# An MLP's first product by seven block products instead of eight, on one core

## The chip, the core and the metric

The program runs on one core of a Trainium2 chip. The metric is the device time of one execution in microseconds (us). The engines named below are PE (TensorE, the matrix multiplier; PEld is its weight load), DVE (VectorE), ACT (ScalarE), POOL (GpSimd) and SP (SyncE, which here only issues DMAs). Each runs its own instructions in order and waits on semaphores for the others. 16 DMA engines move the data, whoever issues a transfer.

## The reference, cut to what matters

The program is two transformer blocks, in float32. The first has two layers, each with a mixer and an MLP. The change touches the MLPs alone:

```python
def squared_relu_mlp(h, w_up, w_down):
    a = jax.nn.relu(jnp.einsum('bld,df->blf', h, w_up))
    return jnp.einsum('blf,fd->bld', a * a, w_down)

# in first_block, once per layer
h = h + squared_relu_mlp(rmsnorm(h, mlp_norm[layer]), w_mlp_up[layer], w_mlp_down[layer])
```

`h` has 528 tokens (16 of them meta tokens) of 1024 features, `w_up` is 1024 x 4096, `w_down` 4096 x 1024. Layer 0 (first mixer: a gated scan over chunks beside latent attention) computes all 528 tokens; in layer 1 (second mixer: a pooling over windows) only 512 are needed.

## The kernel before, in words

Everything is held transposed: features on the 128 partitions, tokens along the free dimension, so `h` is eight tiles of 128 x 528. A float32 product is made of three float32r products: an operand is split into `hi` (a rounding cast, on ACT) and `lo` (the rest, `x - hi`, on DVE), and hi x hi, hi x lo and lo x hi are accumulated in PSUM. `split` (L258 to L262) does this for weights: `whi` is written at L259 and `wlo` at L260.

The weights of all products lie in one packed DRAM tensor, `stream`, in pieces of 512 KB (eight 128 x 128 blocks). `hu` (L212) loads a piece from the SP queue (`load`, L253) into one of three `raw` buffers and splits it into one of three `whi` and three `wlo` buffers. `dense` (L270, its matmuls at L289) multiplies a piece with `xh` and `xl`; with 528 tokens each weight block is used for two halves of 264 columns (`pm`, a pair of PSUM banks), with 512 tokens for one matmul of 512 columns (`ps`).

`mlp` (L1082) runs once per layer. It splits the eight tiles of `h` into `xh` and `xl` (`xsplit`, L466 and L467), starts the first two column blocks of `w_up`, and computes the rms row `rb` beside them (`rms`, L413 and L417; the row is made at L427 to L453). Then four groups run: eight column blocks of `w_up` (32 in all), each followed by ReLU times `rb` on DVE (L1108), a square on ACT (L1112) and a split into `ah` and `al`, and then eight column blocks of `w_down`, whose results are added to `h` on DVE (L1121). For layer 1 the tiles of `h` are first finished by `pool_band` (L1184 ff.), one tile at a time.

Layer 0's mixer (`layer0`, L574) is woven of threads in six phases (`WEAVES`). At the start of the second phase POOL fetches a table of masks, `msk` (L634), DVE turns it into bytes (L635), and each of the four scan heads uses it (`att_level`, L561). POOL also clears a few tiles in this stage (L514, L945, L1063, L1069).

A scheduler places the instructions of each engine: program order is only a priority, and an instruction that is ready goes ahead of an earlier one that is not.

## Time and profile before

| | us |
|---|---|
| median of 3 runs | 1750.56 (1749.06 to 1750.74) |
| the profiled execution | 1750.7 |
| its span, first to last instruction | 1748.8 |
| layer 0's MLP, from its first full column block to the last group's end | 341.6 to 711.2 |
| layer 1's MLP, the same | 749.2 to 1102.2 |

The profile's page gives busy times of the engines over the whole span. Its views by stage are the chain of work that ended last (what ended each wait, followed back from the end), the table of busy times in stretches of the span, the timeline of an engine (start, duration, tile written and tiles read), the groups of like instructions with their count and mean duration, and the DMA queues and transfers of a stretch. The granted clock of PE is 1.00 (2.4 GHz) through both MLPs.

### The profile page before, as it was taken

The page shows a single profiled execution, that of the slowest core. Times are in us where ns is not written, and L with a number is a line of the kernel's source. Part 1 is how long each engine was busy: PE and PEld are TensorE (multiplying, and loading weights), DVE is VectorE, ACT ScalarE, POOL GpSimd, SP SyncE. Part 2 cuts the span into 40 slices and gives each one's busy share as a digit, 9 for nine tenths or more (in the row PEclk, how much of TensorE's full clock was granted, in tenths as well). Part 3 has the DMA queues.
Part 4 walks back from the last instruction along what each step waited for, and adds up shares of the span by engine and source line. Part 5 has one row for each costly group of instructions (what it writes and reads, how often), then busy time and mean ns, then how long its engine had stood idle before and what let it go on. Part 6 is the DMA issues. An engine that isn't in the chain of part 4 may idle for free.

```text
span 1748.8 us, 26901 instructions
## 1 busy us (share of the span) xinstructions
PE 1700.9 (97%) x10674; PEld 1494.4 (85%) x10674; DVE 1090.7 (62%) x1885; ACT 860.5 (49%) x1419; POOL 54.5 (3%) x66
## 2 busy tenths in 40 slices
PE   8999999999999999999999999999999999999996
PEld 7999999999999999878888888767767788888884
DVE  7677675643434344553434345589867768999996
ACT  5456654432323133541413134454346359999995
POOL 0000000000000000000000000100000000101111
PEclk9999999999999999999999999999989999999999
DMA  5211113332323232133333334322201468999994
GB/s 190 70 50 49 37 37 106 85 96 86 94 88 94 89 91 79 61 91 93 94 97 96 96 97 135 111 73 73 73 13 55 160 224 292 348 339 377 374 375 136
DMA packets 72482, 228.42 MB, mean 131 GB/s; under 512 B 8456, under 2 KB 8512, under 8 KB 72352
## 3 DMA queue, kind: packets, MB, share of 16 engines
q1 hardware_dynamic: 69120, 216.22, 36.4%
q0 software_dynamic: 3232, 10.44, 3.0%
q8 instruction: 85, 1.39, 0.3%
q14 instruction: 45, 0.37, 0.1%
HBM read 213.50 MB, written 13.12 MB: 130 GB/s over the span
## 4 chain that ended last, share of the span: by engine, by line
PE 92%; DVE 5%; ACT 2%; issue 1%; DMA 0%; SPq 0%; POOL 0%; POOLq 0%; DVEq 0%; ACTq 0%
PE pm L289 32%; PE ps L289 29%; PE ps L1591 7%; PE ps L1571 3%; PE ps L266 3%; PE ps L267 2%; PE ps L268 2%; PE ps L557 2%; PE ps L2062 1%; DVE wlo L260 1%; PE ps L2037 1%; PE ps L1192 1%; PE pm L485 1%; PE ps L2055 1%; DVE acc L1837 1%
## 5 line engine op out<-in xcount | busy, mean ns | idle before, releaser
L259 ACT CAST whi<-wraw 128x1024 fp32r<-128x1024 f32 (+1 forms) x309 | 321.3, 1045 | 606.6 <-PE pm L289 293.1
L260 DVE TENSOR_TENSOR wlo<-wraw,whi 128x1024 fp32r<-128x1024 f32 (+1 forms) x309 | 373.4, 1217 | 42.5 <-ACT whi L259 32.3
L289 PE MATMUL pm<-xh,whi 128*128 128x264 f32 x976 | 202.2, 288 | 8.7 <-ACT whi L259 5.9
L289 PE MATMUL pm<-xh,wlo 128*128 128x264 f32 x976 | 200.9, 287 | 0.5 <-DVE wlo L260 0.5
L289 PE MATMUL pm<-xl,whi 128*128 128x264 f32 x976 | 200.6, 287 | 0.0
L289 PE MATMUL ps<-xh,whi 128*128 128x512 f32 x472 | 192.1, 407 | 0.0
L289 PE MATMUL ps<-xh,wlo 128*128 128x512 f32 x472 | 186.2, 395 | 0.0
L289 PE MATMUL ps<-xl,whi 128*128 128x512 f32 x472 | 185.5, 393 | 0.0
L289 PEld LDWEIGHTS pm<-xh,whi 128*128 128x128 f32 x976 | 152.8, 190 | 9.8 <-ACT whi L259 5.9
L289 PEld LDWEIGHTS pm<-xh,wlo 128*128 128x128 f32 x976 | 152.7, 190 | 0.8 <-DVE wlo L260 0.7
L289 PEld LDWEIGHTS pm<-xl,whi 128*128 128x128 f32 x976 | 152.2, 189 | 0.4 <-DVE xl L467 0.3
L289 PEld LDWEIGHTS ps<-xh,whi 128*128 128x128 f32 x472 | 89.3, 189 | 23.6 <-issue 1.8
L289 PEld LDWEIGHTS ps<-xh,wlo 128*128 128x128 f32 x472 | 89.1, 189 | 21.0
L289 PEld LDWEIGHTS ps<-xl,whi 128*128 128x128 f32 x472 | 89.3, 189 | 19.4 <-issue 0.5
L1591 PE MATMUL ps<-wlo,xg 128*128 128x512 f32 x256 | 103.8, 406 | 1.7 <-DVE wlo L260 1.6
L289 PE MATMUL pm<-ah,whi 128*128 128x264 f32 x512 | 104.2, 285 | 0.0
L289 PE MATMUL pm<-ah,wlo 128*128 128x264 f32 x512 | 104.0, 285 | 0.0
L1591 PE MATMUL ps<-whi,xg 128*128 128x512 f32 x256 | 103.7, 405 | 0.0
L289 PE MATMUL pm<-al,whi 128*128 128x264 f32 x512 | 103.7, 284 | 0.0
L289 PE MATMUL ps<-ah,whi 128*128 128x512 f32 x256 | 101.1, 395 | 0.0
L289 PE MATMUL ps<-ah,wlo 128*128 128x512 f32 x256 | 101.0, 394 | 0.0
L289 PE MATMUL ps<-al,whi 128*128 128x512 f32 x256 | 100.5, 393 | 0.0
(501 smaller groups left out, 3202.4 us busy)
## 6 DMA issues: line engine op xcount, KB each, us to landing
wraw<-in_stream_dram SPq DMA_DIRECT2D x306, 512.0 KB, 3.6
t<-in_stream_dram SPq DMA_DIRECT2D x90, 256.0 KB, 6.9
h<-in_stream_dram SPq DMA_DIRECT2D x37, 512.0 KB, 6.0
h<-in_xT_dram SPq DMA_DIRECT2D x16, 264.0 KB, 4.3
hd<-h SPq DMA_DIRECT2D x8, 256.0 KB, 2.0
h<-hd SPq DMA_DIRECT2D x8, 256.0 KB, 4.2
out_dram<-t SPq DMA_DIRECT2D x8, 256.0 KB, 2.3
gt<-rbd POOLq DMA_DIRECT2D x4, 256.0 KB, 5.6
```

The costliest lines, as they stand in the source:

```text
L259: self.nc.scalar.copy(hi, src)
L260: i = self.nc.vector.tensor_sub(lo, src, hi.bitcast(F32))
L266: nc.tensor.matmul(ps, wh, xh, start=start, stop=False)
L267: nc.tensor.matmul(ps, wh, xl, start=False, stop=False)
L268: nc.tensor.matmul(ps, wl, xh, start=False, stop=stop)
L289: nc.tensor.matmul(ps, w[:, b, :], x[:, sl], start=(first and f and i == 0), stop=(last and l and i == nb - 1))
L485: nc.tensor.matmul(pm[:, s, :H2], l, r[:, s * H2:(s + 1) * H2], start=i == 0, stop=i == len(pairs) - 1)
L557: nc.tensor.matmul(pa[:, j * 64:(j + 1) * 64], xs, self.second(xs, i), start=True, stop=True)
L1192: nc.tensor.matmul(ps[:, i * 128:i * 128 + n], self.z[:, i, cols], self.bands[i][:, g, :n], start=False, stop=i == NT - 1, skip_group_chec ...
L1571: nc.tensor.matmul(pg[:, j * m:(j + 1) * m], src[2 * i + k // 4][:, sl], oh[:, i, :m], start=i == 0, stop=i == NT - 1, skip_group_check=True)
L1591: nc.tensor.matmul(pa, xk, v[:, k], start=kk == 0 and n == 0, stop=kk == 7 and n == 1, skip_group_check=True)
L1837: nc.vector.match_replace(out=acc, in_to_replace=m8, in_values=acc, imm_value=sel)
```

## The change

The up-product of each MLP is computed by one level of Strassen's scheme. Features, columns and tokens are halved: for each pair of column blocks (16 pairs of 2 x 128 columns) the eight block products of (half of the features) x (half of the tokens) become seven, of which three use a plain quarter of `w_up` and four use a sum or difference of quarters. One such product (`up_prod`) is 12 matmuls of 264 columns (256 in layer 1).

- The four sums of weights (`up_sums`) are formed in a DRAM tensor for all pairs at once, by DMAs that POOL issues: four copies of a quarter (4 MB each), then four DMAs that add into them, some of which read the result of an earlier one. Layer 0's are written into the program at the starts of the mixer's second to fifth phase, layer 1's at the starts of the four groups of layer 0's MLP.
- `up_weights` loads the seven operands of each pair from the two DRAM tensors in pieces of 256 KB, two to a `raw` buffer, and splits them as before.
- `up_x` makes the seven token-side operands (scaled halves of `h`, their sums and differences), each split into `hi` and `lo`, in four steps between which the first pair's products are issued.
- `pair` runs seven products in two to four PSUM banks. Partial sums that several outputs need are copied out of the accumulating bank by ACT while the bank goes on accumulating, and are added on DVE.
- `dense` puts the two halves of 264 columns in two single banks, since layer 0's MLP now runs with eight single PSUM banks. `w_down` is multiplied as before.

```diff
-N_DENSE = 198
+N_DENSE = 198 - 2 * 32
+UP_PARTS = (("w", 0), ("s", 0), ("s", 1), ("w", 1), ("s", 2), ("s", 3), ("w", 3))
+PAIRS = 16
 def pack_stream(i, hus):
...
+def pack_up(w):
+    v = w.reshape(2, 4, 128, PAIRS, 2, 128)
+    return np.ascontiguousarray(v.transpose(4, 0, 3, 2, 1, 5)).reshape(4, PAIRS, 128, 4, 128)
 def shape_consts():
...
+        elif n == T and self.p_pm is None:
+            res = [self.psb()[:, :H2] for _ in range(2)]
+            parts = [(res[s], slice(s * H2, (s + 1) * H2)) for s in range(2)]
...
+        self.ups = {}
+        sums = self.up_sums(0)
...
                     nc.gpsimd.dma_start(msk, self.a["msk"])
                     nc.vector.tensor_copy(self.msk, msk)
+                if n:
+                    next(sums, None)
                 self.weave(*[(thread(th), m) for th, m in ws])
...
+    def up_sums(self, layer):
+        up = self.a["up%d" % layer]
+        s = self.ups[layer] = self.p_d.tile([4, PAIRS, 128, 4, 128], F32, name="ups%d" % layer)
+        for j, q in ((0, 2), (2, 0), (1, 0), (3, 1)):
+            self.nc.gpsimd.dma_start(s[j], up[q])
+        yield
+        for some in (((0, up[3]), (2, up[2])), ((1, s[0]),), ((3, s[1]),)):
+            for j, src in some:
+                self.nc.gpsimd.dma_start(s[j], src, accum_op=OP.add, max_dma_last_dim=8192)
+            yield
+    def up_weights(self, layer):
+        src = {"w": self.a["up%d" % layer], "s": self.ups[layer]}
+        seq = [(t, q, p) for p in range(PAIRS) for t, q in UP_PARTS]
+        for j in range(0, len(seq), 2):
+            raw = self.p_raw.tile([128, 8, 128], F32, name="wraw")
+            for b in range(2):
+                t, q, p = seq[j + b]
+                self.nc.sync.dma_start(raw[:, 4 * b:4 * b + 4], src[t][q, p])
+            hi = self.p_whi.tile([128, 8, 128], F32R, name="whi")
+            lo = self.p_wlo.tile([128, 8, 128], F32R, name="wlo")
+            self.split(hi, lo, raw)
+            for b in range(2):
+                yield hi[:, 4 * b:4 * b + 4], lo[:, 4 * b:4 * b + 4]
+    def up_x(self, pa, h, gname, n, ready):
+        nc = self.nc
+        hn = n // 2
+        x = {p: [None] * 4 for p in range(7)}
+        left = []
+        def half():
+            if not left:
+                big = len(self.bx) < 8
+                t = [(self.p_x if big else pa).tile([128, T], F32R, name=nm if big else "b" + nm, bufs=None if big else 6)
+                     for nm in ("xh", "xl")]
+                self.bx.append(t)
+                left.extend([[v[:, s * hn:(s + 1) * hn] for v in t] for s in range(2)])
+            return left.pop(0)
+        def put(p, k, src, scale=None):
+            hi, lo = half()
+            if scale is None:
+                nc.scalar.copy(hi, src)
+                nc.vector.tensor_sub(lo, src, hi.bitcast(F32))
+            else:
+                nc.scalar.activation(hi, src, AF.Copy, scale=scale)
+                nc.vector.scalar_tensor_tensor(lo, src, scale, hi.bitcast(F32), op0=OP.mult, op1=OP.subtract)
+            x[p][k] = hi, lo
+        self.bx = []
+        tops, bots, n6 = {}, {}, {}
+        for k in range(4):
+            ready(k)
+            b = tops[k] = pa.tile([128, T], F32, name="ah")[:, :n]
+            nc.scalar.activation(b, h[k], AF.Copy, scale=self.vec(gname, k))
+            put(0, k, b[:, :hn])
+        yield x
+        for k in range(4):
+            b = tops[k]
+            nc.vector.tensor_sub(b[:, :hn], b[:, :hn], b[:, hn:])
+            put(1, k, b[:, :hn])
+        for k in range(4):
+            ready(4 + k)
+            b = bots[k] = pa.tile([128, T], F32, name="al")[:, :n]
+            nc.scalar.activation(b, h[4 + k], AF.Copy, scale=self.vec(gname, 4 + k))
+            t = tops[k]
+            nc.vector.tensor_add(t[:, :hn], t[:, :hn], b[:, hn:])
+            put(2, k, t[:, :hn], -1.0)
+        yield x
+        for k in range(4):
+            put(3, k, bots[k][:, :hn])
+        for k in range(4):
+            t = tops[k]
+            nc.vector.tensor_sub(t[:, hn:], bots[k][:, hn:], t[:, hn:])
+            put(4, k, t[:, hn:])
+        yield x
+        for k in range(4):
+            put(5, k, bots[k][:, hn:])
+        for k in range(4):
+            t = tops[k]
+            nc.vector.tensor_sub(t[:, :hn], t[:, :hn], bots[k][:, :hn])
+            put(6, k, t[:, :hn])
+        yield x
+    def up_prod(self, ps, w, x, hn, first, last):
+        nc = self.nc
+        (hi, lo) = next(w)
+        for k, (xh, xl) in enumerate(x):
+            for v, y, f, l in ((hi, xh, True, False), (hi, xl, False, False), (lo, xh, False, True)):
+                nc.tensor.matmul(ps, v[:, k, :], y, start=first and f and k == 0, stop=last and l and k == 3, skip_group_check=True)
     def mlp(self, h, layer, n, ready=lambda c: None, done=lambda c: None):
         nc, tc = self.nc, self.tc
+        hn = n // 2
         with ExitStack() as es:
-            pa = es.enter_context(tc.tile_pool(name="mlp", bufs=12))
+            pa = es.enter_context(tc.tile_pool(name="mlp", bufs=8))
             b8 = list(range(8))
-            up = [self.hu(cols("up%d" % layer, j * 128)) for j in range(3)]
-            xh, xl = self.xsplit(h, "mlp%d" % layer, n, ready)
-            w = [up.pop()]
-            up[0] = self.dense(up[0], b8, xh, xl, n)
-            acc = self.dense(up[1], b8[:4], xh[:4], xl[:4], n, None, True, False)
-
-            def rest():
-                up[1] = self.dense(up[1], b8[4:], xh[4:], xl[4:], n, acc, False, True)[0]
-
-            rb, _ = self.rms(h, n, rest)
-            rbv = self.v2(rb) if n == T else rb
+            w = self.up_weights(layer)
+            xs = self.up_x(pa, h, "mlp%d" % layer, n, ready)
+            def pair(x):
+                u, c = (self.psb()[:, :hn] for _ in range(2))
+                p1, q = self.tmp(n), self.tmp(n)
+                p1sb, usb, u7sb = p1[:, :hn], p1[:, hn:], q[:, :hn]
+                prod = lambda ps, p, f, l: self.up_prod(ps, w, x[p], hn, f, l)
+                prod(u, 0, True, False)
+                nc.scalar.copy(p1sb, u)
+                yield
+                prod(c, 1, True, True)
+                prod(u, 2, False, False)
+                nc.scalar.copy(usb, u)
+                yield
+                a = self.psb()[:, :hn]
+                prod(a, 3, True, True)
+                prod(u, 4, False, False)
+                nc.scalar.copy(u7sb, u)
+                t = [self.tmp(n) for _ in range(2)]
+                nc.vector.tensor_add(t[0][:, :hn], a, p1sb)
+                nc.vector.tensor_add(t[0][:, hn:], c, usb)
+                nc.vector.tensor_add(t[1][:, hn:], c, u7sb)
+                yield
+                d = self.psb()[:, :hn]
+                prod(d, 5, True, True)
+                prod(u, 6, False, True)
+                nc.vector.tensor_add(t[0][:, hn:], d, t[0][:, hn:])
+                def rest(rb):
+                    rbv = [rb[:, s * hn:(s + 1) * hn] for s in range(2)]
+                    stt = nc.vector.scalar_tensor_tensor
+                    stt(t[1][:, :hn], u, 0.0, rbv[0], op0=OP.min, op1=OP.mult)
+                    stt(t[1][:, hn:], t[1][:, hn:], 0.0, rbv[1], op0=OP.min, op1=OP.mult)
+                    stt(t[0], t[0], 0.0, rb, op0=OP.max, op1=OP.mult)
+                    for v in t:
+                        b = self.tmp(n)
+                        nc.scalar.activation(b, v, AF.Square)
+                        hi = pa.tile([128, T], F32R, name="ah")[:, :n]
+                        lo = pa.tile([128, T], F32R, name="al")[:, :n]
+                        self.split(hi, lo, b)
+                        ah.append(hi)
+                        al.append(lo)
+                yield rest
+            x, it, rb = None, None, None
+            sums = iter(()) if layer else self.up_sums(1)
             for g in range(4):
+                next(sums, None)
                 ah, al = [], []
-                for j in range(8):
-                    if up:
-                        pm = up.pop(0)
+                for j in range(4):
+                    if it is None:
+                        it = x and pair(x)
+                    if g == 0 and j == 0:
+                        for _ in range(4):
+                            x = next(xs)
+                            if _ == 0:
+                                it = pair(x)
+                            rest = next(it)
+                        it = None
+                        def mid():
+                            nonlocal it
+                            it = pair(x)
+                            for _ in range(2):
+                                next(it)
+                        rb, _ = self.rms(h, n, mid)
                     else:
-                        pm = self.dense(w.pop(0) if w else self.hu(cols("up%d" % layer, (g * 8 + j) * 128)), b8, xh, xl, n)
-                    t = self.tmp(n)
-                    tv = self.v2(t) if n == T else t
-                    nc.vector.scalar_tensor_tensor(tv, pm, 0.0, rbv, op0=OP.max, op1=OP.mult)
-                    if g == 0 and j == 1:
-                        w.append(self.hu(cols("up%d" % layer, 384), pin=True))
-                    a = self.tmp(n)
-                    nc.scalar.activation(a, t, AF.Square)
-                    hi = pa.tile([128, T], F32R, name="ah")[:, :n]
-                    lo = pa.tile([128, T], F32R, name="al")[:, :n]
-                    self.split(hi, lo, a)
-                    ah.append(hi)
-                    al.append(lo)
+                        for rest in it:
+                            pass
+                        it = None
+                    rest(rb)
                 for c in range(8):
                     pm = self.dense(self.hu(cols("down%d" % layer, c * 128, 8, g * 8)), b8, ah, al, n)
-                    hk = self.v2(h[c]) if n == T else h[c]
-                    nc.vector.tensor_add(hk, hk, pm)
+                    for hk, p in zip([h[c][:, :hn], h[c][:, hn:]], pm) if n == T else [(h[c], pm)]:
+                        nc.vector.tensor_add(hk, hk, p)
                     if g == 3:
                         done(c)
             return
         with self.tc.tile_pool(name="pool", bufs=1) as p:
             self.pool_begin(p)
+            self.banks(0, 8)
             self.mlp(self.h, 0, T, done=self.pool_part)
             for k in range(8):
                 self.dump("h_mlp0", self.h[k], lambda d, k=k: d[:, k, :])
             if self.stop == "mlp0":
                 return
             self.pool_layer(p)
-            self.banks(0, 8)
             hr = [self.h[k][:, NM:] for k in range(8)]
             self.mlp(hr, 1, S, ready=self.pool_band)
         for k in range(8):
```

## Rows read from the trace of the kernel before

**Rows 1.** The page's head: span, then busy time (share of the span).
```profile
span 1748.8 us, 26901 instructions
PE 1700.9 (97%) x10674; PEld 1494.4 (85%) x10674; DVE 1090.7 (62%) x1885; ACT 860.5 (49%) x1419; POOL 54.5 (3%) x66
```
**Rows 2.** Chain that ended last, in order of time: start, duration, what.
```profile
341.64 338.96 PE pm L289 x2784
...
749.23 352.96 PE ps L289 x1524
```
**Rows 3.** By stretch: busy PE, PEld, DVE, ACT, POOL; clock, DMA share, GB/s.
```profile
322.00:341.50 19.50, 18.05 (x150) 17.81 (x148) 14.99 (x28) 12.13 (x19) 0.00 (x0) 1.00 0.20 55
341.60:386.50 44.90, 44.86 (x369) 44.89 (x370) 21.80 (x25) 17.03 (x23) 0.00 (x0) 1.00 0.33 97
386.50:433.20 46.70, 46.70 (x387) 46.70 (x386) 16.15 (x17) 9.63 (x10) 0.00 (x0) 1.00 0.30 91
...
735.30:749.20 13.90, 12.83 (x61) 10.08 (x60) 9.40 (x19) 7.70 (x13) 0.00 (x0) 1.00 0.00 1
```
**Rows 4.** PE's timeline (start, duration): matmuls of 264, 512 and 256 columns.
```profile
459.95 0.41 PE L289 MATMUL pm<-xh,whi 128*128 128x264 f32 x2
...
469.69 0.41 PE L289 MATMUL pm<-xl,whi 128*128 128x264 f32 x2
...
799.72 0.39 PE L289 MATMUL ps<-ah,whi 128*128 128x512 f32 x1
...
807.81 0.39 PE L289 MATMUL ps<-ah,wlo 128*128 128x512 f32 x1
...
711.27 0.28 PE L266 MATMUL ps<-whi,xh 128*128 128x256 f32 x1
...
714.13 0.28 PE L266 MATMUL ps<-whi,xh 128*16 128x256 f32 x1
```
**Rows 5.** Groups by line and form, DVE then ACT: count, busy us, mean ns.
```profile
L260 DVE TENSOR_TENSOR wlo<-wraw,whi 128x1024 fp32r<-128x1024 f32 x306 | 371.3, 1222 | 40.8 <-ACT whi L259 30.5
...
L260 DVE TENSOR_TENSOR al<-t,ah 128x528 fp32r<-128x528 f32 x32 | 22.7, 708 | 0.5
...
L532 DVE TENSOR_TENSOR t<-c,b 128x264 f32<-128x264 f32 x16 | 7.0, 440 | 0.0
...
L259 ACT CAST whi<-wraw 128x1024 fp32r<-128x1024 f32 x306 | 319.5, 1049 | 605.2 <-PE pm L289 293.1 <-PE ps L289 264.7 <-issue 36.1
...
L259 ACT CAST ah<-t 128x528 fp32r<-128x528 f32 x32 | 20.3, 635 | 1.0
...
L1820 ACT ACTIVATE t<-ps 128x256 f32<-128x256 f32 x8 | 2.7, 379 | 2.2 <-PE ps L268 2.2
```
**Rows 6.** DMA issues, us to landing: layer 0's MLP (341:711), then the experts (1450:1740).
```profile
wraw<-in_stream_dram SPq DMA_DIRECT2D x64, 512.0 KB, 3.5
...
wraw<-in_stream_dram SPq DMA_DIRECT2D x93, 512.0 KB, 8.8
```
**Rows 7.** DMA queues in 1450:1740: packets, MB, share of 16 engines (q0 adds into DRAM).
```profile
q1 hardware_dynamic: 29927, 87.99, 79.5%
q0 software_dynamic: 2176, 7.93, 14.4%
```
**Rows 8.** Busy times by stretch, as rows 3: the program's first 54 us.
```profile
3.00:54.00 51.00, 46.36 (x343) 44.90 (x344) 36.84 (x59) 26.87 (x44) 0.01 (x1) 1.00 0.53 175
```
**Rows 9.** POOL's timeline: start, duration, line, operation.
```profile
2.06 0.73 POOL L1639 DMA_DIRECT2D slot<-in_slot_dram  x1
2.79 0.22 POOL L514 MEMSET v<- 128x128 f32 x1
54.63 0.60 POOL L634 DMA_DIRECT2D t<-in_msk_dram  x1 [51.62 <-PE pm L485]
```
**Rows 10.** DVE's timeline: the masks turned to bytes, and their first use.
```profile
69.11 0.36 DVE L635 CAST msk<-t 128x384 uint8<-128x384 f32 x1
...
83.27 0.74 DVE L561 COPY_PREDICATED at<-msk,ps 128x256 f32<-128x256 uint8 x1
```

3 lines of the change are left out of this document (2 added, 1 removed).

## The prediction

> **What bounds the kernel now.** I read the busy times first: PE is busy for 97% of the span [rows 1], and the 1.9 us by which the execution (1750.7) exceeds its span lie outside it; it stands 0.14 above the median, so sums against it need no correction. Then the chain that ended last, in order of time: through both MLPs it is one piece of matmuls each, 339 and 353 us long [rows 2]. No wait ends late there. The busy times by stretch say the same for one group of layer 0's MLP: PE 44.9 of 44.9 us in the eight up blocks and 46.7 of 46.7 in the down blocks, at granted clock 1.00, while DVE has 21.8 and 16.2, ACT 17.0 and 9.6, and the DMA engines a third [rows 3]. So a matmul removed there is worth its full spacing, as long as DVE, ACT and the transfers, which get more to do, stay below PE.
>
> **What is removed.** Spacings come from PE's timeline. 264 columns: from 459.95 to 469.69 lie 40 pairs, 121.75 ns each matmul. 512 columns: 35 from 799.72 to 807.81, 231.1 ns. 256 columns: 24 from 711.27 to 714.13, 119.2 ns [rows 4]. Layer 0's up-product is 32 blocks x 48 matmuls = 1536 of 264 columns; seven products of 12 for 16 pairs are 1344. 192 x 121.75 ns = **23.4 us**. Layer 1's is 32 x 24 = 768 of 512 columns, 177.5 us; it becomes 1344 of 256 columns, 160.2 us: **17.3 us**, less because each half-width matmul brings its own weight load and costs more than half. Together 40.7 us: 1710.0 if nothing else moved.
>
> **What is added in the steady groups.** By durations of [rows 5]: DVE has 1.22 us for a 1024-wide split, 0.71 for 528, 0.44 for 264; ACT 1.05, 0.64 and (256 from PSUM) 0.38. A pair needs 3.5 weight splits instead of 2. DVE: 3.5 x 1.22 + four additions and two half-width ReLUs x 0.44 + one ReLU and two splits x 0.71 = 9.0 us. ACT: 3.5 x 1.05 + three copies x 0.38 + four x 0.64 = 7.4 us. PE has 84 x 121.75 ns = 10.2 us (10.0 in layer 1). DVE fits with 12% to spare; before it had 49% of the stretch [rows 3]. The cover is thin, and there is a short-fused step: ACT must copy the accumulating bank while PE does the 12 matmuls of another product, 1.46 us. Behind a 1.05 us cast the copy ends after 1.43 us plus two semaphores; the trace shows no such case. Bounds: nothing, or 0.2 us x 3 copies x 32 pairs = 19 us. I take 3, nearer to nothing, because ACT is free for a quarter of the time.
>
> **What is added at each start-up.** All seven token-side operands must exist before the first pair is through: 28 half-width splits and 16 half-width sums on DVE, 44 x 0.44 = 19.4 us, plus 1.8 for the pair's additions, for eight full splits x 0.71 = 5.7. In layer 0 DVE was busy 15.0 of 19.5 us at this point and PE idle for 1.45 [rows 3]: 15.0 - 5.7 + 19.4 + 1.8 = 30.5 us on DVE. PE has 18.05 plus 2.9 (seven products and the three put beside the rms row, 14.6 us, for two blocks, 11.7): 20.9. So some 9.6 us idle for 1.45, 8 us more. Layer 1 has the same operands and only 1.1 us of slack in its 13.9 [rows 3]; again 8. Bounds for each: 2 us, if the rms sums and the next pair fill in, and 13 if nothing does. I take 16 for both.
>
> **The transfers.** A quarter of w_up is 4.19 MB. The trace has no DRAM to DRAM copy of this size. Its nearest rows are loads and adding DMAs among the experts: 79.5% of 290 us for 87.99 MB is 2.6 us per MB with all 16 engines, 14.4% for 7.93 MB is 5.3 [rows 7]. So four copies take 44 to 88 us; four adds, which read twice, 88 to 177. The Trainium skill, page "DMA: Bandwidth & Descriptors", section "Latency and other measured facts", gives 207 to 214 GB/s for copies between HBM tensors; by that four would be about 80 us, an estimate, inside these bounds. When do they start? The copies read only inputs, and POOL is idle from 3 to 54 us; a transfer that the program has after both MLPs, of the slot table, was issued at 2.06 us [rows 9]. So I expect all copies that nothing holds back at about 3 us, wherever the program has them. There they meet the first loads, 53% of the engines for 51 us [rows 8]. PE waits for those loads at the start: 0 to 15 us (twice the time for the first 15), and I take 4, as the copies' packets need only share.
>
> **The sum.** 1750.7 - 40.7 + 3 + 16 + 4 = **1733 us**, own range 1714 (start-ups at 2 us, nothing else) to 1745.
>
> **Rivals.** (1) *The masks queue behind the copies; slower.* POOL's transfers all run on one software queue, q0 [rows 7]. The masks are fetched on it at 54.6 us; DVE casts them at 69.1, and the first scan head uses them at 83.3 [rows 9, 10]. DVE works in order, so behind a late mask stand the weight splits, and PE stops within two or three pieces. If the copies of both layers are issued at 3 us, the masks land after 2.8 + 27 (0.53 x 51, the other loads) + 88 to 177 = 118 to 207 us: 35 to 124 us late, 1768 to 1857 altogether, middle 1812. It decides from the point where more than 80 us of transfers stand ahead of the masks; four copies alone give 74 to 118, from nothing to 35. For it: the slot table's row, which shows how far an unhindered transfer moves up, and the idle POOL. Against it: no row shows two large transfers of POOL at once, so that one holds the other back is not seen; and the scan heads could be placed later. The Trainium skill, the same page, section "SWDGE vs HWDGE vs iDMA", states that one queue only is allocated for transfers issued by GpSimd; by that rule the masks come behind every byte of the copies, and this rival holds. The trace agrees in that it has no other software queue than q0. The adds belong here too: POOL waits in order for a copy before it issues the add, and the clears for the scan heads stand behind it.
> (2) *Loads pace the up groups.* A piece now lasts 24 x 121.75 ns = 2.92 us instead of 5.84. With three raw buffers one cycle is landing + cast + split: 3.5 + 1.05 + 1.22 = 5.8 us for three pieces, within 8.8. While the DMA engines are full, landing took 8.8 us [rows 6], the cycle is 11.1, a piece 3.7: 0.77 x 14 = 11 us for each group of layer 0's MLP in which layer 1's sums run. One to three such groups beside the sum: 1744 to 1766.
> (3) *The sums come late.* At the upper ends (177 + 177 us, and the mixer's loads) layer 0's last sum ends behind 330 us, where the MLP begins: up to 75 us, 1733 to 1808.
> (4) *It doesn't do what it says*: a matmul of 256 or 264 columns held up by its own weight load would lose the gain. At 119 and 122 ns [rows 4] the spacing still follows the columns, so nearly excluded.
>
> **How the numbers follow.** Forecast 0.42, rival 1 0.33, rival 2 0.17, rival 3 and the rest 0.08. This measurement can tell 0.2%, 3.5 us, from no change. Faster: the forecast but for 0.01, and 0.04 of rival 2, 0.45. Same: 0.07, mostly rival 2. Slower: 0.33 + 0.07 + 0.08 = 0.48. The likeliest case is faster though slower has the larger sum, since slower is spread over three mechanisms. The range goes from the forecast's low end, 1714, up to 1835, which leaves out rival 1's upper fifth and a little of rival 3.
>
> **What would show it.** Right: about 10 us of PE per pair and no wait inside the groups; 8 us more of PE waits on DVE (token-side operands) at each start; the copies on POOL's timeline before 10 us. Rival 1: DVE's cast of the masks late by tens of us and waiting for a DMA, PE idle between 70 and 200 us. Rival 2: SP's loads landing after 6 us and more in layer 0's up groups, PE waiting for the cast of weights. Rival 3: PE idle at the first product with a sum, SP waiting for POOL's adds. The forecast is wrong if PE's idle time grows by over 37 us anywhere.

## The result and the profile after

The changed kernel takes **1859.9 us** (median, 1858.8 to 1865.7) beside 1749.8 for the kernel before on the same chip: ratio 1.064, 95% interval 1.061 to 1.066. The prediction said 1733 us, in a range of 1714 to 1835. Its sign, its size and its range were wrong.

The page of the changed kernel (profiled execution, span 1858.5 us), to be read against [rows 1]:

```profile
PE 1715.5 (92%) x11058; PEld 1527.6 (82%) x11058; DVE 1208.5 (65%) x2197; ACT 948.5 (51%) x1619; POOL 67.1 (4%) x82
...
PE   6979899955999999996999999999999999999996
...
PEclk9988898976999999997999999999999999999998
DMA  7649576599434344312444435431220358999994
...
q1 hardware_dynamic: 92160, 241.40, 38.5%
q0 software_dynamic: 8096, 77.55, 16.7%
...
PE 81%; DMA 7%; DVE 6%; ACT 3%; issue 1%; SPq 0%; POOL 0%; ACTq 0%; DVEq 0%; POOLq 0%
```

In the PE line the holes stand in slices 1, 3 and 9 to 10 (of 46.5 us each). The DMA line shows 7 to 9 tenths in slices 1, 9 and 10, but only 4 in slice 3. The granted clock shows 8 tenths or less in six of the first ten slices. The last line is the chain by engine: transfers are now 7% of it. The chain in order of time (start, duration, what) names them:

```profile
2.60 16.50 DMA h<-in_xT_dram
...
71.03 27.28 DMA wraw<-in_stream_dram
...
362.06 21.56 DMA wraw<-ups
...
386.43 33.38 DMA wraw<-in_up_dram
...
426.35 14.35 DMA wraw<-ups
...
455.80 12.59 DMA wraw<-ups
...
536.88 41.65 PE ps L1195 x336
578.53 46.72 PE ps L303 x384
625.25 41.65 PE ps L1195 x336
666.90 46.72 PE ps L303 x384
...
948.15 40.87 PE ps L1195 x336
989.02 44.70 PE ps L303 x192
```

Two things are to be seen. The steady groups gained what they should: 336 matmuls of an up group in 41.65 us where 384 took 46.6. And all of that is small beside waits for loads of some 256 KB that take 12 to 33 us, at the start, once in the mixer (from 71 us) and at the start of layer 0's MLP, where the kernel before landed 512 KB in 3.5 us [rows 6]. Between 100 and 355 us, though, the chain holds no DMA at all.

I cut both traces at the same places: the first and the last matmul of the down groups (those that read `ah` or `al`), from PE's timeline. Times in us from the span's start; the last two columns are experiments that come below.

| | before | after | no sums | paced, down pieces |
|---|---|---|---|---|
| layer 0: first down group starts | 376.7 | 486.5 | 385.8 | 375.8 |
| it ends | 423.6 | 536.9 | 436.1 | 422.6 |
| each later up group | 46.6 | 41.5 | 41.5 | 41.4 |
| last down group ends | 711.4 | 810.3 | 709.5 | 695.8 |
| layer 1: first down group ends | 826.9 | 948.2 | 841.7 | 811.5 |
| each later up group | 44.2 | 40.7 | 40.7 | 40.7 |
| last down group ends | 1093.9 | 1204.8 | 1098.4 | 1067.2 |
| span ends | 1748.8 | 1858.5 | 1754.5 | 1717.2 |

109.8 us are lost before the first down group. (The 1102.2 us given ahead of the prediction as the end of layer 1's MLP include 8 us of a product that comes behind its last down group.) POOL's transfer of the band, which stands at the mixer's end, was issued at 294.1 us before and at 354.9 after: 61 us of the loss lie up to there, in the program's start and the mixer, and 49 at the start of layer 0's MLP.

Where the sums were issued is on POOL's timeline (start, duration, tile written and read, what ended the idle time before):

```profile
1.46 0.73 POOL L1105 DMA_DIRECT2D ups<-in_up_dram  x1
65.80 0.61 POOL L650 DMA_DIRECT2D t<-in_msk_dram  x1 [63.61 <-PE pm L499]
66.40 1.50 POOL L1105 DMA_DIRECT2D ups<-in_up_dram  x3
...
138.06 2.14 POOL L1109 DMA_DIRECT2D ups<-in_up_dram  x2
...
163.99 1.01 POOL L1109 DMA_DIRECT2D ups<-ups  x1 [11.55 <-DMA ups<-in_up_dram]
...
356.51 2.17 POOL L1109 DMA_DIRECT2D ups<-in_up_dram  x2
396.44 1.01 POOL L1109 DMA_DIRECT2D ups<-ups  x1 [37.76 <-DMA ups<-in_up_dram]
397.06 0.97 POOL L1801 DMA_DIRECT2D slot<-in_slot_dram  x1
440.51 1.04 POOL L1109 DMA_DIRECT2D ups<-ups  x1 [42.48 <-DMA ups<-ups]
```

Only one copy went to the start. Three more followed the masks at 66 us, because POOL stood in order behind the masks' transfer, which waited for PE to free its tile. The masks landed after 2.7 us. Layer 1's adds ran from 356 us on, over the start of layer 0's MLP. The busy times of the stretches (length, busy us of PE, PEld, DVE, ACT, POOL with instructions, mean granted clock of PE, share of the DMA engines, GB/s):

```profile
70.00:100.00 30.00, 19.50 (x150) 18.32 (x149) 9.11 (x13) 6.47 (x9) 0.00 (x0) 0.91 1.04 352
100.00:150.00 50.00, 46.76 (x339) 44.97 (x339) 37.58 (x84) 25.50 (x44) 4.82 (x8) 0.88 0.49 136
150.00:200.00 50.00, 48.64 (x314) 44.99 (x314) 30.28 (x71) 27.76 (x60) 1.21 (x2) 0.87 1.04 230
200.00:250.00 50.00, 45.07 (x320) 42.98 (x320) 28.55 (x66) 23.11 (x53) 1.19 (x5) 0.86 0.30 87
...
350.00:400.00 50.00, 38.27 (x292) 37.40 (x292) 17.05 (x29) 15.85 (x26) 5.34 (x7) 0.91 0.88 231
400.00:450.00 50.00, 20.96 (x93) 18.78 (x93) 22.78 (x47) 16.17 (x35) 1.04 (x1) 0.60 0.99 225
```

Where a sum runs, the DMA engines are full. PE stands beside it from 70 to 100 us and from 400 to 450, but not from 150 to 200. PE's granted clock lies below 1.00 in every stretch from 70 to 300 us, part of each at 1.2 GHz, where the kernel before had 1.00 up to 700 us. Up to the band's transfer PE's idle time grew by 34.8 us, and the lower clock, 0.86 to 0.91 over 230 us, accounts for about 29 more: an estimate from the stretches, near the 61 us that were lost up to there.

Not all of this loss falls beside transfers. In one stretch of the mixer no packet of the sums moves and the loads take a tenth of the DMA engines, and PE still does only 212 matmuls in 36.5 us; the kernel before did 408 of its own in 50 (second row):

```profile
208.50:245.00 36.50, 31.57 (x212) 29.48 (x211) 18.25 (x50) 14.36 (x39) 0.38 (x3) 0.81 0.10 29
```

```profile
200.00:250.00 50.00, 49.95 (x408) 48.58 (x407) 37.64 (x93) 28.25 (x68) 1.02 (x5) 1.00 0.14 43
```

What differs there is the order of the program. Each engine runs its instructions in order, so a trace shows the order that the scheduler made. Up to the band, PE's matmuls (by text of the line and tile) stand in one and the same order in the kernel before and in the runs below without sums, with a plain first group, and paced. The changed kernel has another one from about 88 us on, and the runs below with the transfers in bursts have it too, those with one layer's sums in parts.

The packets of the trace say how a load was held back. A 4.19 MB copy goes as 64 packets of 65,536 bytes, 3.0 us each in the mean (2.8 in the first copy, 3.1 from 71 to 98 us); an add as 512 packets of 8 KB, 0.63 us each; a load's packets have 2 or 4 KB and take 0.084 to 0.098 or 0.16 us. From 390 to 430 us q0, the sums' queue, and q1, the loads', have 952 packets each (some of 4 bytes included): by these counts each DMA engine takes one of the one and one of the other, however long they are. The Trainium skill, page "DMA: Bandwidth & Descriptors", section "Queues, rings and completion order", says so too: an engine goes round its queues and drains a whole packet before it switches; the counts of this stretch agree. So beside an add a load of 2 KB packets gets 0.098 of each 0.726 us, 13% of the engine, beside a copy 3%; both are worked out from the packets' times. The program's start does not show such turns: from 2.6 to 15.0 us 64 packets of the first copy and 317 of the loads passed.

### The profile page after: what moved, and what is told of

It reads as the page before. It is cut to its first block, busy times and chain, and to the rows that moved or that the text cites. A ratio compares the mean times of both kernels' runs of the same rounds, so it can differ in the third digit from the quotient of the medians.

```text
span 1858.5 us, 28619 instructions
## 1 busy us (share of the span) xinstructions
PE 1715.5 (92%) x11058; PEld 1527.6 (82%) x11058; DVE 1208.5 (65%) x2197; ACT 948.5 (51%) x1619; POOL 67.1 (4%) x82
## 3 DMA queue, kind: packets, MB, share of 16 engines
q0 software_dynamic: 8096, 77.55, 16.7%
## 4 chain that ended last, share of the span: by engine, by line
PE 81%; DMA 7%; DVE 6%; ACT 3%; issue 1%; SPq 0%; POOL 0%; ACTq 0%; DVEq 0%; POOLq 0%
PE ps L303 28%; PE ps L1195 16%; PE pm L303 7%; PE ps L1753 6%; PE ps L1733 3%; DMA wraw<-ups 3%; PE ps L277 2%; PE ps L278 2%; PE ps L279 2%; DMA wraw<-in_up_dram 2%; PE ps L571 2%; DMA wraw<-in_stream_dram 1%; DVE wlo L271 1%; ACT whi L270 1%; PE ps L2224 1%
## 5 line engine op out<-in xcount | busy, mean ns | idle before, releaser
L303 PE MATMUL ps<-ah,whi 128*128 128x264 f32 (+1 forms) x768 | 205.5, 322 | 1.1 <-ACT whi L270 1.1
L303 PE MATMUL ps<-ah,wlo 128*128 128x264 f32 (+1 forms) x768 | 204.7, 321 | 0.0
L303 PE MATMUL ps<-al,whi 128*128 128x264 f32 (+1 forms) x768 | 204.4, 320 | 0.0
L1195 PE MATMUL ps<-xh,whi 128*128 128x264 f32 (+1 forms) x512 | 153.8, 302 | 32.4 <-ACT whi L270 10.7
L1283 DVE TENSOR_TENSOR h<-h,ps 128x264 f32<-128x264 f32 (+1 forms) x96 | 46.6, 513 | 200.5 <-PE ps L303 200.5
L1195 PE MATMUL ps<-xl,whi 128*128 128x264 f32 (+1 forms) x512 | 150.9, 295 | 0.0
L1195 PE MATMUL ps<-xh,wlo 128*128 128x264 f32 (+1 forms) x512 | 149.3, 295 | 0.2
L303 PEld LDWEIGHTS ps<-ah,whi 128*128 128x128 f32 x768 | 127.5, 188 | 12.9 <-ACT whi L270 1.5
L303 PEld LDWEIGHTS ps<-ah,wlo 128*128 128x128 f32 x768 | 127.2, 188 | 11.5
L303 PEld LDWEIGHTS ps<-al,whi 128*128 128x128 f32 x768 | 127.3, 188 | 11.3
L1195 PE MATMUL ps<-bxh,whi 128*128 128x264 f32 (+1 forms) x384 | 113.0, 294 | 10.4 <-ACT bxh L1147 6.3
```

The costliest lines, as they stand in the source:

```text
L303: nc.tensor.matmul(ps, w[:, b, :], x[:, sl], start=(first and f and i == 0), stop=(last and l and i == nb - 1))
L1195: nc.tensor.matmul(ps, v[:, k, :], y, start=first and f and k == 0, stop=last and l and k == 3, skip_group_check=True)
L1283: nc.vector.tensor_add(hk, hk, p)
```

## The experiments

The theory at first (T): the sums' transfers hold the loads back packet by packet, and what the seven products gain is as forecast. Rivals: bandwidth alone counts (R1); the MLP itself loses, or the order that the scheduler makes of the mixer (R2); the lower clock is the cause (R3).

**No sums at all.**

```diff
-        sums = self.up_sums(0)
+        sums = iter(())
...
-            sums = iter(()) if layer else self.up_sums(1)
+            sums = iter(())
...
-        src = {"w": self.a["up%d" % layer], "s": self.ups[layer]}
+        src = {"w": self.a["up%d" % layer], "s": self.a["up%d" % layer]}
```

> The changed kernel without any of the 16 DMAs that form the sums; where a product takes a sum it reads a plain quarter of the same layer's w_up, of the same size, so the output is not the reference's, and every other instruction stays. Theory T (the sums' DMAs hold back the loads of the program's start, of the mixer and of the start of layer 0's MLP, and the Strassen products themselves gain what was forecast): the 110 us of loss go, 1722 to 1740 us. Rival R2 (the Strassen MLP itself loses, by its start-ups, the load on DVE or the order that the scheduler makes of the mixer): the time stays above 1800 us. Rival R3 (the loss is a lower granted clock, from the work itself): above 1800 us too, with the stretches of lower granted clock between 105 and 300 us kept.

Measured: 1755.3 us, ratio 1.0025 (1.0015 to 1.0035). With the sums' transfers 104.6 us go, and the lower clock up to 300 us goes with them (0.96 and more): that the MLP itself loses is out for the loss as a whole, and so is R3. The mixer's order is not out, since this run has the order of the kernel before again; transfers and order went together. And the time lies 15 us above the upper end expected: the MLP without any sums gains nothing by itself.

**One layer's sums alone.** (`sums = iter(())` at one of the two places.)

> The changed kernel with layer 0's eight sum DMAs alone; layer 1's products read plain quarters instead of sums, so the output is not the reference's. Theory T: the 61 us that the mixer lost (11.2 up to the masks, 25.7 up to the clear of the second scan head, 24.0 up to the band's load) stay, less the part that layer 1's copies at 245 to 290 us had, and the 44 us at the start of layer 0's MLP go: 1770 to 1800 us. R2: as the changed kernel, 1850 to 1860.

> The changed kernel with layer 1's eight sum DMAs alone; layer 0's products read plain quarters instead of sums, so the output is not the reference's. Theory T: the four copies read inputs alone, and POOL is free, so some of them move up into the mixer, and the adds fall on the start of layer 0's MLP or before it: the 44 us there stay in part, the mixer's loss is that of at most four copies; 1750 to 1800 us. R2: as the changed kernel, 1850 to 1860.

Measured: 1810.8 (1.0345; 1.0328 to 1.0362) and 1800.6 (1.0290; 1.0263 to 1.0318). Against the run without sums, layer 0's cost 55 us and layer 1's 45, 101 of the 104.6 together. That is no proof that each layer's loss is its own: 55.0 of the one and 41.1 of the other fall before the band's transfer (last table of this section), while with both together 59.5 fall there and 41.3 at the start of layer 0's MLP. Both lie at or above the ends expected, since the base was 1755 and not 1733.

**The kernel before, with the sums beside it.**

```diff
         self.o = h
+        self.ups = {}
+        sums = self.up_sums(0)
...
+                if n:
+                    next(sums, None)
...
+            sums = iter(()) if layer else self.up_sums(1)
             for g in range(4):
+                next(sums, None)
```

> The kernel before, with its own MLPs, and beside it the 16 DMAs that form the sums, at the same places of the program; nobody reads the sums. Theory T: the loss without the gain, 1750 + 61 in the mixer + 25 to 45 at the start of layer 0's MLP = 1835 to 1860 us. R2: the DMAs beside other work cost little, 1750 to 1775 us.

Measured: 1819.5 (1.0389; 1.0371 to 1.0406), 68.5 us of loss instead of 104.6; the expectation's lower end was 15 us too high. The difference lies at the start of layer 0's MLP: from the band to the first down group 90.6 us here (82.7 in the kernel before), 131.6 in the changed kernel (90.3 without sums). With the old up groups beside the same sums PE stays busy, at the same DMA share:

```profile
350.00:400.00 50.00, 45.06 (x351) 44.85 (x351) 23.66 (x30) 18.14 (x25) 5.32 (x7) 0.93 0.96 260
400.00:450.00 50.00, 48.35 (x396) 47.85 (x395) 24.03 (x36) 18.39 (x26) 1.04 (x1) 1.00 0.98 240
```

An old up group asks for a third of the DMA engines [rows 3], an up group of seven products for 0.52 (from 424.9 to 466.3 us of the run with a plain first group, below). The old group's loads have packets of 4 KB, 0.173 us, which beside an add makes a share of 22% instead of 13%. So what the loads want counts beside what their turns leave them.

**Shorter packets.**

```diff
-            self.nc.gpsimd.dma_start(s[j], up[q])
+            self.nc.gpsimd.dma_start(s[j], up[q], max_dma_last_dim=8192)
```

> The changed kernel; only the eight copies' packets are made 8 KB long instead of 64 KB, as the adds' already are. Bytes, order and destinations stay. Theory T (turns: a load's packet waits for one packet of the sums on each DMA engine, 2.96 us for 64 KB, some 0.4 us for 8 KB at the same rate): the part of the loss that stems from the copies goes nearly all, the adds' part stays: 1790 to 1830 us, the first load lands in under 8 us instead of 16.5, a 512 KB load beside copies in under 8 us instead of 27. Rival R1 (the share of bandwidth counts, so bytes alone): as the changed kernel, 1850 to 1865 us.

The second run has `max_dma_last_dim=2048` for copies and adds; in the trace the copies' packets then have 4 KB and the adds' 2 KB.

> The changed kernel with packets of 2 KB for the eight copies and the eight adds alike. Theory T: a load's packet waits some 0.1 us behind a copy's and 0.15 us behind an add's, so it keeps about half of each engine: the loss of 105 us shrinks to 15 to 45, 1770 to 1800 us. Rival R1 (bytes): 1850 to 1865 us. In between or slower: the small packets make the sums themselves longer, which their landing times then show.

Measured: 1856.5 (1.0609; 1.0582 to 1.0636) and 1825.2 (1.0438; 1.0404 to 1.0472). The first fell where R1 had put it, the second between the two theories. T in its first form, that the copies' long packets are the fault, has fallen: with a copy's packet at 0.31 us the start of the program, the mixer and the start of layer 0's MLP (131.3 us for 131.6) stayed nearly as they were. Short packets for the adds as well changed one stage: from the band to the first down group it took 102.7 us. There a load gets 0.098 of 0.274 us beside an add, about a third, where a steady group of seven products wants 0.52. So at the start of layer 0's MLP the turns do count, and it was the adds that held the loads back. The mixer's loss does not follow the packets: the band was issued at 349.6 and 346.9 us, beside 354.9 in the changed kernel and 295.5 without sums; the mixer's order is that of the changed kernel in both. q0's share of the 16 engines is 16.7% of 1858.5 us against 3.0% of 1754.5 without sums: 258 us of all engines for the 16 transfers.

**A plain first group.** The first of the four groups is done as in the kernel before, and the seven token-side operands are formed beside it.

```diff
             for g in range(4):
...
-                for j in range(4):
+                for j in range(8 if g == 0 else 4):
+                    if g:
+                        for rest in pair(x):
+                            pass
+                        rest(rb)
+                        continue
+                    if up:
+                        pm = up.pop(0)
                     else:
+                        pm = self.dense(pw.pop(0) if pw else self.hu(cols("up%d" % layer, j * 128)), b8, xh, xl, n)
...
+                    x = next(xs)
```

> No sums' DMAs, as in the run without sums, and the first of the four groups of each MLP is computed as in the kernel before, by eight full column blocks; the seven token-side operands are formed during that group, and the other three groups take the seven products, with plain quarters in place of sums (the output is not the reference's). Theory S: the two starts cost 16.2 and 20.3 us instead of 8 each, since PE stands idle for 8.7 us in each and then runs for a while at half the granted clock; both go with a plain first group, and three groups of each layer keep the gain seen in the run without sums, 5.1 and 3.5 us each: 1751 - 25.8 = 1725 us, within 5. Rival S2 (the missing gain lies in the steady groups or in the shared PSUM banks): 1740 us or more.

Measured: 1723.8 (0.9844; 0.9820 to 0.9868), on the expected 1725. The two starts, from 325 us and from the end of layer 0's last down group, both to the next down group, in the run without sums (first two rows) and in this one:

```profile
325.00:385.80 60.80, 49.48 (x354) 46.86 (x352) 48.53 (x100) 38.40 (x74) 0.00 (x0) 0.89 0.35 113
709.50:793.70 84.20, 69.94 (x476) 65.44 (x474) 57.64 (x121) 48.43 (x95) 0.00 (x0) 0.86 0.26 81
```

```profile
325.00:378.00 53.00, 51.88 (x426) 51.55 (x425) 41.13 (x81) 33.89 (x59) 0.00 (x0) 1.00 0.30 90
698.10:769.30 71.20, 67.52 (x356) 57.77 (x355) 50.64 (x95) 43.05 (x76) 0.00 (x0) 0.95 0.22 67
```

PE's idle time of 11.3 and 14.3 us became 1.1 and 3.7, and the granted clock went from 0.89 and 0.86 to 1.00 and 0.95, for the same operands made on DVE a little later.

**Work for PE while it waits at the starts**, to part the lower clock from the idle time.

```diff
             x[p][k] = hi, lo
+            for _ in range(2):
+                nc.tensor.matmul(fill, hi[:, :128], hi, start=True, stop=True, skip_group_check=True)
```

> The run without sums, with two more matmuls of 264 (256) columns after each of the 28 token-side operands of a start, which write to a bank that nobody reads: work for PE while it waits for operands, 6.8 us at each start. Theory S2 (a good half of the lost time at the starts is half clock that follows PE's idle time, not the idle time itself): granted clock there rises towards 1.00, the 6.7 and 8.6 us of half-clock loss go, PE's wait for operands stays; some of the added matmuls cost time: 1738 to 1750 us. Rival (the lower clock comes from something else, or costs nothing): the clock stays at 0.7 to 0.9 there and the time at 1755 us or above.

Measured: 1757.4 (1.0029; 1.0017 to 1.0040), no gain over the run without sums. The clock rose, from 0.90 to 0.98 in the 25 us from 325 and from 0.69 to 0.89 from 740 to 760, so work on PE raised it. But the added matmuls took as much time as they gave back: the first down group of layer 0 started 2.0 us earlier, of which 1.7 lie before the band, and the gap before layer 1's was 2.5 us longer. What the clock alone costs at the starts is therefore not shown; only that idle time and lower clock go together when PE has real work.

**The sums made by POOL in SBUF.** The first group plain, four plain quarters loaded for each pair, four additions of 128 x 512 on POOL.

```diff
-                self.nc.sync.dma_start(raw[:, 4 * b:4 * b + 4], src[t][q, p])
+            add(s[:, :4], b[:, :4], b[:, 4:])
+            add(s[:, 4:], a[:, :4], s[:, :4])
+            add(t[:, :4], a[:, :4], b[:, 4:])
+            add(t[:, 4:], a[:, 4:], s[:, 4:])
```

> The first group of each MLP plain, as in the run above, and the sums right, formed on the chip: the four plain quarters of a pair are loaded (1 MB for 1.75), and POOL, idle in both MLPs, makes the four sums in SBUF, 128 x 512 each. No trace of this case shows such an addition on POOL. If one takes up to 2.5 us, four fit beside a pair's 10.4 us on PE: 1725 to 1735 us, below both kernels. Rival: they are slower or hold DVE up, the three up groups of a layer become longer than 41.6 and 40.8 us and PE waits for the cast of weights: above 1750 us.

Measured: 1742.3 (0.9954; 0.9936 to 0.9973): below the kernel before, but 18 us above the run with a plain first group and no sums. The additions fit (by shape: count, busy us, mean ns), but DVE pays. First POOL in this run, then two groups of DVE in it, then the same DVE group where POOL is idle (the run with a plain first group):

```profile
L1113 POOL TENSOR_TENSOR wsum<-wraw,wsum 128x512 f32<-128x512 f32 x24 | 42.0, 1750 | 1.4
...
L1112 POOL TENSOR_TENSOR wsum<-wraw 128x512 f32<-128x512 f32 x24 | 36.6, 1524 | 574.6 <-DMA wraw<-in_up_dram 561.3 <-DVE wlo L273 13.3
```

```profile
L273 DVE TENSOR_TENSOR wlo<-wraw,whi 128x512 fp32r<-128x512 f32 x27 | 31.1, 1153 | 32.4 <-ACT whi L272 32.4
...
L273 DVE TENSOR_TENSOR al<-t,ah 128x528 fp32r<-128x528 f32 x32 | 30.2, 972 | 0.7 <-ACT ah L272 0.5
```

```profile
L273 DVE TENSOR_TENSOR al<-t,ah 128x528 fp32r<-128x528 f32 x32 | 21.5, 702 | 2.4 <-ACT ah L272 2.3
```

A subtraction on DVE of two SBUF operands takes 972 ns on average beside POOL's additions and 702 without; the 128 x 512 ones on `wraw` 1153, where one beside an idle POOL took 0.69 us (at 462.7 us of this run). DVE's operations with a PSUM operand keep their 0.42 us. Each later up group took 43.4 to 45.0 us instead of 41.4 and 40.7, PE waiting for `wlo`. The Trainium skill, page "SBUF — State Buffer", section "SBUF: two separate sides", agrees: a DVE operation with two SBUF inputs and a GpSimd one that reads SBUF lock each other out.

**Bursts against pacing.** Two runs with the true sums by DMAs, a plain first group (so 12 of 16 pairs need sums) and short packets. In the first the transfers stand where the changed kernel has them.

> Right sums by DMAs again, in the places of the changed kernel (bursts of four transfers and more), with the short packets (copies 4 KB, adds 2 KB), for the 12 of 16 pairs that are needed when the first group of each MLP is plain. It is the partner of the paced run. Without the sums this form took 1723.8 us. The run with short packets lost 1825 - 1755 = 70 us to the sums; three quarters of that are 52, less something because a plain first group asks for 0.30 of the DMA engines instead of 0.54: 1760 to 1780 us by both theories below.

In the second one pair's four copies or four adds (256 KB each) are released at a time. POOL copies one column of a piece's `wlo`, and the transfers are queued behind that copy:

```diff
+    def pace(self, lo, every):
+        self.paced += 1
+        if self.sums is None or self.paced <= 0 or self.paced % every:
+            return
+        g = self.nc.gpsimd.tensor_copy(self.tick, lo[:, 0, 0:1].bitcast(F32)).ins
+        with self.tc.issue_after(g):
+            if next(self.sums, 0) == 0:
+                self.sums = None
```

> As the run with bursts and a plain first group: same bytes, same packets, same 12 pairs, but one pair's four copies or four adds (256 KB each) at a time, released after a weight piece's split on DVE: one step behind each of 31 pieces of the mixer for layer 0, behind every second piece of layer 0's MLP for layer 1. Theory B (what costs is a burst longer than the three raw buffers cover: loads get a half to a third of the engines for tens of us): nearly all of the loss goes, 1724 to 1738 us. Theory E (the engines' time that the sums take is lost whenever it falls, some 200 us of all 16): as with bursts, 1760 to 1780 us.

Measured: 1781.3 (1.0159; 1.0138 to 1.0180) in bursts, **1735.9** (0.9909; 0.9889 to 0.9929) paced. The same bytes in the same packets cost 57 us over the run without sums in the one form and 12 in the other. So the engines' time is not lost by itself (theory E). Theory B is not shown by this pair. The two runs part before the band's transfer, issued at 349.7 us in bursts and at 295.6 paced, and there the bursts come with the changed kernel's order of the mixer, the paced steps with the old one. From the band to the first down group the run with bursts took 82.6 us, the paced one 82.5, the kernel before 82.7, although the bursts filled the DMA engines all that time. This is that stretch with bursts, and then the changed kernel's:

```profile
349.70:432.40 82.70, 81.58 (x671) 81.26 (x670) 53.25 (x95) 41.65 (x69) 8.94 (x8) 1.00 1.01 243
```

```profile
354.90:486.50 131.60, 89.45 (x593) 85.59 (x592) 60.20 (x113) 47.39 (x88) 6.38 (x8) 0.78 0.93 232
```

With a plain first group the loads want 0.30 of the engines, and packets of 4 KB (0.173 us) beside adds of 0.178 could have about half.

The 12 us that were left lie in two up groups of layer 0's MLP beside which steps ran (first two rows below; 48.2 and 46.8 us for 41.5). The last run releases none there:

```diff
-            self.pace(lo, self.every)
...
-                self.paced, self.every, self.sums = 0, 2, self.up_sums(1)
+                self.paced, self.sums = 0, self.up_sums(1)
```

> The paced run with one change: in layer 0's MLP a step of layer 1's sums is released behind every full piece (first group and down blocks) and none behind the weights of the seven products. In the paced run the two up groups beside which steps ran took 48.2 and 46.8 us for 41.5, at a DMA share of 1.02 and 0.96, while the down groups beside steps kept 46.9 at 0.60 and 0.73. Theory B (a transfer costs where loads and sums together fill the engines, and nothing elsewhere): the 12 us go, 1723 to 1729 us. Rival (the steps, now one behind every 5.8 us, fill the engines in the down groups instead): down groups above 47.5 us, 1734 us or more.

Measured: **1721.0** (0.9832; 0.9815 to 0.9848), 2 us below the expectation; the down groups keep 46.9 us. The two up groups in the paced run, and then the first of them and the down group behind it in this one:

```profile
425.00:473.10 48.10, 43.28 (x336) 42.32 (x335) 30.80 (x48) 24.64 (x38) 22.00 (x35) 0.96 0.94 266
520.00:566.80 46.80, 43.36 (x338) 42.59 (x337) 30.68 (x48) 24.85 (x38) 18.61 (x31) 0.96 0.92 271
```

```profile
422.60:464.00 41.40, 41.40 (x337) 41.06 (x336) 30.60 (x48) 24.66 (x38) 3.27 (x5) 1.00 0.54 165
464.00:510.90 46.90, 46.90 (x388) 46.90 (x387) 18.12 (x28) 10.74 (x13) 20.87 (x36) 1.00 1.00 281
```

The expectation's theory, that a transfer costs where loads and sums together fill the engines, had the time right and the reason wrong: the down group kept PE busy throughout at a DMA share of 1.00, and the rival's condition came true without its cost. (The shares of 1.02 and 0.96 quoted there belong to stretches that reach into the down groups.) What the up and down groups differ in is what their loads want, 0.54 and about 0.30.

Queue q0 still takes 15.8% of 1717.2 us, 271 us of all engines and 219 of them for the sums, at no cost that can be seen. Against the kernel before, layer 1's last down group ends 26.6 us earlier (first table: 1.0 up to the first down group, 14.6 up to layer 0's end, 11.0 in layer 1). The other 4.9 us lie behind both MLPs, where nothing was changed; they were not looked into.

**All runs by stage.** Times in us. "Order" is PE's order of matmuls in the mixer: old is that of the kernel before. "Turns" is a load's share beside an add, worked out from the packets' times, where adds ran behind the band. A steady up group of seven products wants 0.52, an old one about a third.

| | order | masks issued | band issued | from the band to the first down group | turns |
|---|---|---|---|---|---|
| before | old | 54.6 | 294.1 | 82.7 | |
| no sums | old | 54.4 | 295.5 | 90.3 | |
| changed kernel | other | 65.8 | 354.9 | 131.6 | 13% |
| layer 0's sums alone | other, in parts | 65.8 | 350.5 | 91.2 | |
| layer 1's sums alone | other, in parts | 66.9 | 336.6 | 93.0 | |
| before, with sums | other | 66.1 | 351.7 | 90.6 | 22% |
| copies of 8 KB | other | 66.8 | 349.6 | 131.3 | 13% |
| all short | other | 65.6 | 346.9 | 102.7 | 36% |
| plain first, no sums | old | 54.5 | 295.6 | 82.4 | |
| plain first, bursts | other | 63.4 | 349.7 | 82.6 | 49% |
| plain first, paced | old | 67.0 | 295.6 | 82.5 | |
| paced, down pieces | old | 66.4 | 293.3 | 82.4 | |

The last two columns go together: the more of an engine the turns leave beside what the loads want, the less is lost. The mixer goes with the order: in the five runs with the changed kernel's order the band was issued at 347 to 355 us, whatever the packets, the MLP behind it or the loads' share. No run has the other order without the transfers, so what the order alone costs is not shown.

## Why the prediction was wrong, point by point

- **What bounds the kernel**: right. PE's chain was tight, so a matmul taken away counted in full in the steady groups, and each wait put in its place too. The stretches read as up and down blocks [rows 3] were cut 10 us late (the first down group ran from 376.7 to 423.6 us); PE is full in the right ones as well.
- **The matmuls removed** (40.7 us) **and the coupling in the pairs** (3): right in kind. Measured 5.1 us for each group of layer 0 and 3.5 of layer 1, 34.4 for eight: 6.3 less than 40.7, so the term of 3 should have been 6. It is no wait for ACT or DVE; PE is busy for all of a group, at 124.0 and 121.6 ns a matmul (41.65 and 40.87 us for 336) instead of 121.75 and 119.2.
- **The start-ups** (8 us each, at most 13): this term was mis-sized. Measured, in the run without sums: layer 0's first group ends 12.5 us later than before, less 1.4 lost in the mixer, plus the 5.1 that it should have saved: 16.2. Layer 1's 16.7 + 3.5 = 20.2. PE's idle time grew by 9.7 and 10.5 us (against the same stretches of the kernel before, which have 1.6 and 3.8), close to the 8 worked out. The lower granted clock, 0.11 of 60.8 us and 0.14 of 84.2 less 3.5 that the kernel before has there, would account for 6.7 and 8.3 more, an estimate that the run with added matmuls did not bear out. The 20 us by which both starts exceed their term make the difference between a small gain and none; a plain first group gave them back.
- **The transfers: the step that failed.** There they "meet the first loads", and the prediction says "I take 4, as the copies' packets need only share". The term counts the copies at the program's start alone; copies and adds beside the mixer and the MLP stand only among the rivals. Sixteen transfers cost 104.6 us. The volume was about right: 64 packets of 2.8 to 3.1 us make 11 to 12 us of all engines for a copy, 45 to 49 for four (44 to 88 expected); 512 packets of 0.63 make 20 for an add, 80 for four (88 to 177). Against the run without sums 11.4 us were lost up to the masks, which is within the bounds given for the program's start (0 to 15). 48.1 were lost from there to the band: one wait of 27.3 us for a load from 71 us on, and then none for a DMA, in another order of instructions. The adding of the sums to the program changed that order, and this the prediction did not consider; how much it costs by itself stays open. 41.3 were lost at the start of layer 0's MLP, and there the runs show the reason: beside an add a load got 13% of an engine, where a group of seven products wants half, and waits for loads held the chain for 12.6 to 33.4 us each.
- **"All copies that nothing holds back at about 3 us"**: wrong. One went there, the rest waited behind the masks on POOL. So the loss came to the mixer and to layer 0's MLP, which had no term of the sum.
- **Rival 1** (masks behind the copies, 1768 to 1857) came nearest in time (its upper end), with a mechanism that did not occur: the masks landed in 2.7 us, as nothing stood ahead of them. Its rule of the one queue did hold elsewhere: the slot table's transfer, issued 0.6 us behind an add at 397 us, landed after 43.4 us. **Rival 2** (loads pace the up groups because the engines are full) had the right mechanism for the start of layer 0's MLP, at 11 us a group; it was worked out for steady groups with landings of 8.8 us, while the sums fell on the first group, where waits for a load took 12 to 33. With short packets and paced, such a group lost 6.7 and 5.3 us. **Rival 3** (late sums): no wait for a sum stood in the chain. **Rival 4**: out, as forecast.
- **The price of a copy** that the Trainium skill gives (page "DMA: Bandwidth & Descriptors", section "Latency and other measured facts": 207 to 214 GB/s, by estimate some 80 us for four) is too high here: a copy issued at 245 us landed in 15.7 us, 267 GB/s, issue and other loads included. The Trainium skill's price is for tiles of 128 rows of 16 KiB with a pitch between them, copied from the sync and scalar queues.
- **The point named beforehand** at which the forecast would be wrong, PE idle by over 37 us more, is what the trace showed.

What stays open: what the mixer's other order costs by itself, and so how much of the 48 us lost there is due to the transfers; and what the lower clock costs by itself (filling PE gave no time back). At the start of layer 0's MLP the share of a turn against the share that the loads want gives the order of the runs, not their sizes.

## What to carry to other kernels

A transfer beside tight loads is not priced by its bytes: compare the share that the loads want in that very stretch with the share that one packet in turn leaves them, which the packets' lengths on both sides set. Engines filled to 1.00 cost nothing here where the loads wanted 0.30 and could have a third or more, and 41 us where they wanted half and could have 13%. The same bytes in pieces of 256 KB, released by the work itself beside loads that want little, cost nothing here. When transfers are added to a program that a scheduler orders, compare the order of the other instructions too, before the loss is put down to the transfers. And make new operands beside a stretch that needs only the old ones.

## What the runs showed of the hardware that I had not expected

- A DRAM to DRAM copy issued by POOL goes as packets of 65,536 bytes, 2.8 to 3.1 us each. With packets of 4 KB its engine time hardly changes: the eight copies took 95.6 us of 16 engines in the changed kernel and 99.9 with all packets short.
- Adding in a DMA costs twice the copy: 0.63 us for 8 KB, where the copy takes 0.31 (median, run with copies of 8 KB).
- From 390 to 430 us one queue's packets passed one for one with the other's, though theirs were four times as long (952 of each); at the program's start they did not (64 and 317).
- Full DMA engines need not cost PE anything: share 1.01 for 82.7 us with PE busy for 81.6 of them, as in the kernel before.
- POOL's additions in SBUF slow DVE's operations on two SBUF operands by 40% on average and leave those with a PSUM operand alone.
